# Up-projection pairs as blocks of seven half-size products in a two-layer encoder kernel

## The chip, the cores and the metric

The kernel runs on one core of one Trainium2 chip. The metric is the device time of one execution in microseconds (us). The core has a matrix engine (TensorE, PE in the profile, with its weight loads as PEld), three engines for elementwise work (VectorE is DVE, ScalarE is ACT, GpSimd is POOL), a queue that issues loads (SyncE, SP), on-chip memory (SBUF, 128 partitions), eight PSUM banks into which PE writes, and 16 DMA engines that move data between HBM and SBUF. The engines run side by side. Each works through its own instructions strictly in program order and waits on semaphores for the others.

## The reference, cut to what matters

Two post-norm layers over 512 tokens of width 1024. In each, a token part (attention, retention, gates, output projection, LN1) is followed by a channel part. The change lies in the channel part alone:

```python
def conv_glu_ffn(x, w_up, conv_w, conv_b, w_down):
    h = x @ w_up                       # (512, 1024) @ (1024, 5632)
    hp = jnp.pad(h, ((0, 0), (1, 1), (0, 0)))
    h = hp[:, :-2] * conv_w[0] + hp[:, 1:-1] * conv_w[1] + hp[:, 2:] * conv_w[2] + conv_b
    a, b = jnp.split(h, 2, axis=-1)
    return (jax.nn.gelu(a) * b) @ w_down
...
    ffn = conv_glu_ffn(x, ...)
    ple = jax.nn.sigmoid(x @ w_ple_gate[i]) * (p[i] @ w_ple_proj[i])
    x = layer_norm(ALPHA * x + ffn + ple, ln2_g[i], ln2_b[i])
```

`D_FF` is 2816, that is 22 tiles of 128 channels for the half `a` and 22 for the half `b`.

## The kernel before, in words

**Products in three parts.** Every f32 operand is kept as two rounded parts, `hi` and `lo` (`split`, L169: ScalarE copies the source into `hi`, VectorE subtracts to get `lo`). A product of two operands is three matmuls, hi·hi, hi·lo and lo·hi (`mm3`, L395).

**The weight stream.** All weights of a layer come as chunks of 128x1024 f32 (512 KB) in the order in which they are used (`Stream`, L275). A chunk is loaded by the SP queue (`fetch`), split by ScalarE and VectorE (`prep`), and used by PE (`get`). `get` splits ahead: up to `deep` (5) chunks beyond the one in use, of which at most three in all lie in the three rotating buffers of the pool `wsplit` (`N_W`), those marked as held lying in the large pool `unit` (30 buffers of 4 KB per partition). So the split of a chunk that lies three places later in those buffers has to wait until PE is done with the chunk in use. Loads are issued `LOOK` (3) chunks further ahead.

**Seven products for eight.** Some projections are computed by a Winograd form of Strassen's scheme: the weight is four blocks a, c, b, d, and seven products (kinds a, c, t1, t2, d, t3, t4) with sums of blocks replace eight. The sums of the weight are made by DMA: POOL issues a transfer that adds the next block onto a raw chunk in SBUF (`add`, L303). A raw chunk passes through a, t1, t2 and t4: each sum is added only after the chunk has been split for the kind before (`prep`, L362). Items marked `sent` (L352) make their `lo` in another way: ScalarE negates `hi`, and a POOL DMA adds the weight onto it. The sums of the activations are made by `vg_sums` (L673) on VectorE and ScalarE, eight `unit` buffers for four sums. In the token part `product_t` (L1078) does such a product in 24 matmuls of 128x256, for the gate blocks; in the channel part before the change, the gate of the per-layer input (`pg`, L1340) and the down projection (`products`, L1436) use the scheme with 128x512 matmuls, and the sums of x made for `pg` are dropped after it.

**The channel part.** The 22 pairs of up tiles come in three segments of 3, 4 and 4 pairs of tile numbers (`SEGS`), so 6, 8 and 8 tiles. For one tile, `up_tile` (L1266) runs two products `gemm_t` (one of half a, one of half b) with 24 matmuls of 128x512 each. After each comes a convolution: ScalarE scales the PSUM result into `ca`, VectorE adds the two neighbours with two instructions of 511 columns. Then ScalarE applies GELU and VectorE multiplies the halves. `up_step` (L1299) makes from two tiles the operands of the down projection: `a11` (128x256, from the even tile), `k2` (128x512, from the odd tile), and in `s_parts` (L1287) the two sums `sa` and `sb`, each split into hi and lo. For the last pair of a segment `s_parts` comes after the first down product (L1568).

After the up tiles of a segment come its seven down products in the order a, c, t1, t2, d, t3, t4, each of 24 matmuls (18 in the first segment), each of which reads one operand of every pair of the segment: a reads `a11` of pairs 0 to 3 in turn, c reads `k2`. Their results are added into the residual tiles `R` by VectorE (`into`).

**What sets the order.** In the channel part all five engines keep program order (`_Ordered.on = set(ORD)`, L1255). An instruction that waits holds up all that stand behind it on its engine. So the place at which the Python code emits an operation is the place at which its engine runs it:

```python
        half = []
        for ab in range(2):
            ps = gemm_t(xs)          # get(): splits of later chunks are emitted here
            ...                      # convolution of this half
```

Of the kernel before, what the change touches and what calls it, by code (L numbers as in the profile page):

```python
# [10 lines left out]
F32R = mybir.dt.float32r  # L11
AF = mybir.ActivationFunctionType
ALU = mybir.AluOpType
# [51 lines left out]
BOUND = ("p0", "t4a", "tr", "t4b", "p1")  # L65
VG_DEEP = 3
VG_EARLY = "d"
VG_HELD = (('0t1', '1t1', '0t2', '0c', '1t2', '1a', '1d', '1t3'), ('0a', '0c', '0t1', '1t1', '1t3', '1t2', '0t3', '0t2', '1d'))


# [46 lines left out]
def trunk(tc, wpack, x_nat, x_tr, head, p_tr, rpb, decay, ln_par, ln_col, conv, cos_t, sin_t, dist, xi_d, zd, mask, ident_d, out):  # L117
# [4 lines left out]
    with ExitStack() as es:  # L122
# [14 lines left out]
        def nm(s):  # L137
            cnt[0] += 1
            return f"{s}_{cnt[0]}"
# [7 lines left out]
        def tmp(s, n=512):  # L147
            return tp.tile([P, n], F32, tag="t", name=nm(s))
# [92 lines left out]
        def pg_items(l):  # L241
# [11 lines left out]
                    n += 1  # L253
            return out

        def plain_items(l, f):

            if f[0] in "qk":
                h = int(f[1])
                cs = [12 * (h // 2) + 8 + 2 * (h % 2) + "qk".index(f[0])]  # L260
            elif f[:2] == "ga":
                cs = [52 + int(f[2])]
            elif f[:2] == "bb":
                cs = [44 + int(f[2])]
            elif f == "vn":
                cs = range(32, 36)
            elif f == "xn":
                cs = []
            elif f[0] == "p":
                cs = [72 + int(f[1])]  # L270
            else:
                cs = [24 + 2 * int(f[2]) + "qk".index(f[1])]
            return [Item("w", (l, c, 0, 1024), 1024) for c in cs]

        class Stream:  # L275


            def __init__(self):
                self.seq = []
                for l in range(DEPTH):  # L280
                    tile = 0
                    plain = lambda c: self.seq.append(Item("w", (l, c, 0, 1024), 1024, pool=up if (l, c) in RESIDENT else None))
                    self.seq += vg_items(l)
                    self.seq += fill_items(l)
                    for c in range(60, 72):
                        plain(c)
                    self.seq += pg_items(l)
                    for s, n in enumerate(SEGS):
                        for c in range(UP0 + 2 * max(tile, PG.count("up")), UP0 + 2 * (tile + 2 * n)):
                            plain(c)  # L290
                        tile += 2 * n
# [362 lines left out]
        for l in range(DEPTH):  # L654
# [608 lines left out]
            for t in range(4):  # L1263
                nc.sync.dma_start(R[t], rscr[l][t * P:(t + 1) * P, :])

            def up_tile(i):  # L1266
                half = []
                for ab in range(2):
                    ps = gemm_t(xs)
                    ci = ab * NF + i  # L1270
                    a = tmp("ca")
                    nc.scalar.activation(a, ps, AF.Identity, bias=cw[:, ci, 3:4], scale=cw[:, ci, 1:2])
                    nc.vector.scalar_tensor_tensor(a[:, 1:], ps[:, :-1], cw[:, ci, 0:1], a[:, 1:], op0=ALU.mult, op1=ALU.add)
                    nc.vector.scalar_tensor_tensor(a[:, :-1], ps[:, 1:], cw[:, ci, 2:3], a[:, :-1], op0=ALU.mult, op1=ALU.add)
                    half.append(a)
                nc.scalar.activation(half[0], half[0], AF.Gelu_apprx_tanh)
                nc.vector.tensor_mul(half[0], half[0], half[1])
                return half[0]

            H1, H2 = slice(0, 256), slice(256, 512)  # L1280
            N1, N2 = slice(0, 512), slice(512, 1024)
            tile = 0
            a11, k2, sa, sb, sums = {}, {}, {}, {}, []
# [14 lines left out]

            def up_step(j, last_pair):  # L1299

                nonlocal tile
                p, g = j // 2, up_tile(tile)
                tile += 1
                if j % 2 == 0:
                    if p % 2 == 0:
                        a11p[0] = up.tile([P, 2, 2, 256], F32R, tag="u", name=nm("a11"))
                    a11[p] = a11p[0][:, p % 2]
                    split(a11[p][:, 0, :], a11[p][:, 1, :], g[:, H1])
                    sums.append([p, g])
# [3 lines left out]
                sums[-1].append(g)  # L1313
                if not last_pair:
                    s_parts(*sums.pop())

            a11p = [None]


            def ple_gate(t, c, src, scale):  # L1320
# [12 lines left out]
            def residual():  # L1333

                while late:
                    t = late.pop(0)
                    nc.scalar.activation(xn[t], xn[t], AF.Copy, scale=ALPHA)
                    nc.gpsimd.dma_start(R[t], xn[t], accum_op=ALU.add)

            def pg():  # L1340
# [6 lines left out]
                for key in PG:  # L1347
# [4 lines left out]
                    for k in S_AT:  # L1352
                        if k == name:
                            r = next(sg)
                            S = r if isinstance(r, dict) else S
                    if key == "up":
                        up_step(ups, False)
                        ups += 1
                        residual()
                        continue  # L1360
# [55 lines left out]
            pg()  # L1416
            st = [sp.tile([P, 2, 6], F32, tag="bn", name=nm("bn")) for _ in range(4)]
            for s, n in enumerate(SEGS):
                for j in range(tile - 2 * sum(SEGS[:s]), 2 * n):
                    up_step(j, j == 2 * n - 1)  # L1420
                    residual()
                fin = s == len(SEGS) - 1
                lhs = {
                    "a": lambda p, h, i: a11[p][:, h, i * P:(i + 1) * P],
# [140 lines left out]
                ws.deep = A_DEEP[s]  # L1565
                product("a", u, True)
                ws.deep = DEEP
                s_parts(*sums.pop())  # L1568
                if fin and not last:
                    ple_in(l + 1)  # L1570
                for i in range(2):
# [100 lines left out]
def _pack(w_in, w_ba, w_bb, w_out, w_up, w_down, w_pg, w_pp):  # L1672
    ch = []
    q_na, k_na, v_na, q_r, k_r, v_r, g_r, ga, gb = np.split(w_in, np.cumsum([512, 512, 512, 512, 512, 1024, 1024, 1024])[:], axis=1)
    vr, gr, qr, kr = _mov(v_r), _mov(g_r), _stat(q_r), _stat(k_r)
    for hp in range(2):
        ch += list(vr[hp]) + list(gr[hp])
        for h in (2 * hp, 2 * hp + 1):
            ch += [qr[h], kr[h]]
    qn, kn = _stat(q_na), _stat(k_na)  # L1680
    for m in range(4):
        ch += [qn[m], kn[m]]
    ch += list(_mov(v_na)[0])
# [10 lines left out]
    for i in range(NF):  # L1694
        ch += [su[i], su[NF + i]]
    ch += _blocks(w_down)
    assert len(ch) == NCH
    return np.stack(ch)
# [69 lines left out]
```

## Time and profile before

| | us |
|---|---|
| median of 3 runs (lowest, highest) | 1680.46 (1680.31, 1680.69) |
| span of the profiled execution (first to last instruction) | 1679.3 |
| PE busy | 1669.5 (99%) |
| VectorE busy | 1228.2 (73%) |
| ScalarE busy | 949.1 (57%) |
| POOL busy | 189.2 (11%) |
| all bytes moved by DMA | 289.68 MB, 172 GB/s on average |

The time of the profiled execution is not measured apart from its span; the span is 1.2 us under the median of the runs, which is what lies around it. The matmuls are pipelined: a record of a 128x512 matmul is 389 ns long, while the next one starts 227 ns after it. So durations of matmuls are not added up here, but starts are compared. On the other engines the records follow one another with little overlap, and a row's duration is close to its cost. "idle before <-" in a row names what ended the engine's wait.

In layer 0 the up tiles of the second segment run from 586 us to 673 us, its down products to 711 us, the up tiles of the third segment to 798 us.

### The profile page before, as it was taken

How to read it: one execution, taken by the hardware profiler on the slowest of the kernel's cores; microseconds unless marked ns; L12 is line 12 of the kernel's file. 1: busy time of each engine (PE TensorE's matmuls, PEld its weight loads, DVE VectorE, ACT ScalarE, POOL GpSimd, SP SyncE). 2: the span in 40 equal slices, each digit the busy share in tenths (PEclk: the TensorE clock that was granted, in tenths of full speed). 3: DMA queues.
4: the chain of work that ended last, by engine and by line, in shares of the span. 5: the costliest groups of instructions: out<-in, count | busy, mean ns of one | idle time of the engine just before them, and what ended most of it. 6: DMA issues, size and time to landing. Idle time of an engine off the chain costs nothing.

```text
span 1679.3 us, 22089 instructions
## 1 busy us (share of the span) xinstructions
PE 1669.5 (99%) x8325; PEld 1418.1 (84%) x8325; DVE 1228.2 (73%) x1857; ACT 949.1 (57%) x1418; POOL 189.2 (11%) x216
## 2 busy tenths in 40 slices
PE   9999999999999999999999999999999999999997
PEld 7889988888888888888888899888888888888886
DVE  6756676776787767757876566877688887676678
ACT  6765676853366535335476647668534574353354
POOL 1111111110200100100112011111002010000003
PEclk9999999999999999999999999999999999999999
DMA  8989666666655535535788795667667565265274
GB/s 303 249 234 233 171 149 139 165 173 223 207 135 161 121 112 163 135 111 172 193 231 219 184 245 163 138 144 170 160 241 225 130 171 126 88 181 132 89 212 101
DMA packets 87530, 289.68 MB, mean 172 GB/s; under 512 B 9984, under 2 KB 14592, under 8 KB 87424
## 3 DMA queue, kind: packets, MB, share of 16 engines
q1 hardware_dynamic: 62512, 199.66, 33.7%
q0 software_dynamic: 24912, 88.62, 30.2%
q8 instruction: 65, 1.06, 0.3%
q14 instruction: 41, 0.34, 0.1%
HBM read 269.36 MB, written 17.30 MB: 171 GB/s over the span
## 4 chain that ended last, share of the span: by engine, by line
PE 99%; DVE 1%; ACT 0%; POOL 0%; issue 0%; DVEq 0%; POOLq 0%; ACTq 0%
PE gt L90 31%; PE u L90 13%; PE v L90 7%; PE gt L397 6%; PE gt L398 6%; PE gt L399 6%; PE w L90 4%; PE gn L399 3%; PE gn L397 3%; PE gn L398 3%; PE x L90 1%; PE u L397 1%; PE u L399 1%; PE u L398 1%; PE gn L90 1%; PE na L1023 1%
## 5 line engine op out<-in xcount | busy, mean ns | idle before, releaser
L90 PE MATMUL gt<-x1t,hi 128*128 128x512 f32 x1408 | 433.5, 389 | 0.0
L90 PEld LDWEIGHTS gt<-x1t,hi 128*128 128x128 f32 x1408 | 264.3, 188 | 55.0
L90 PE MATMUL gt<-x1t,lo 128*128 128x512 f32 x704 | 274.1, 389 | 0.1
L90 DVE TENSOR_TENSOR lo<-raw,hi 128x1024 fp32r<-128x1024 f32 (+1 forms) x147 | 175.9, 1206 | 43.5 <-ACT hi L90 43.3
L90 DVE SCALAR_TENSOR_TENSOR ca<-gt,cw,ca 128x511 f32<-128x511 f32 x176 | 131.8, 749 | 78.5 <-ACT ca L90 75.4
L90 ACT CAST hi<-raw 128x1024 fp32r<-128x1024 f32 (+1 forms) x147 | 151.1, 1037 | 33.1 <-PE u L90 13.4
L90 PEld LDWEIGHTS gt<-x1t,lo 128*128 128x128 f32 x704 | 132.2, 188 | 28.1 <-DVE lo L90 1.0
L90 DVE TENSOR_TENSOR lo<-rawa,hi 128x1024 fp32r<-128x1024 f32 x94 | 109.8, 1176 | 49.3 <-ACT hi L90 48.9
L90 ACT ACTIVATE ca<-gt,cw 128x512 f32<-128x512 f32 x88 | 68.5, 779 | 131.7 <-PE gt L90 131.7
L90 ACT CAST hi<-rawa 128x1024 fp32r<-128x1024 f32 x94 | 94.3, 1014 | 39.0 <-DMA rawa<-in_wpack 16.5
L90 POOL DMA_DIRECT2D rawa<-in_wpack x72 | 65.0, 947 | 368.6 <-DVE lo L90 308.0
L397 PE MATMUL gt<-xt,hi 128*128 128x512 f32 x256 | 100.8, 394 | 0.0
L398 PE MATMUL gt<-xt,hi 128*128 128x512 f32 x256 | 99.8, 390 | 0.0
L399 PE MATMUL gt<-xt,lo 128*128 128x512 f32 x256 | 99.7, 389 | 0.0
L170 ACT CAST hi<-raw 128x1024 fp32r<-128x1024 f32 x44 | 45.8, 1050 | 76.2 <-PE gt L398 29.8
L355 ACT CAST hi<-raw 128x1024 fp32r<-128x1024 f32 x48 | 50.4, 1050 | 49.1 <-PE gt L398 41.2
L357 POOL DMA_DIRECT2D lo<-in_wpack x48 | 42.1, 876 | 294.7 <-ACT lo L356 215.4
L90 POOL DMA_DIRECT2D rawt<-in_wpack x20 | 18.8, 1004 | 381.0 <-DMA rawt<-in_wpack 364.8
L171 DVE TENSOR_TENSOR lo<-raw,hi 128x1024 fp32r<-128x1024 f32 x44 | 53.4, 1223 | 10.9 <-ACT hi L170 10.7
L399 PEld LDWEIGHTS gt<-xt,lo 128*128 128x128 f32 x256 | 48.1, 188 | 10.3
L90 PE MATMUL v<-hi,sa 128*128 128x512 f32 x176 | 56.1, 389 | 0.0
L397 PEld LDWEIGHTS gt<-xt,hi 128*128 128x128 f32 x256 | 48.2, 188 | 9.1
(348 smaller groups left out, 4216.9 us busy)
## 6 DMA issues: line engine op xcount, KB each, us to landing
raw<-in_wpack SPq DMA_DIRECT2D x235, 512.0 KB, 3.7
rawa<-in_wpack POOLq DMA_DIRECT2D x84, 512.0 KB, 6.6
lo<-in_wpack POOLq DMA_DIRECT2D x48, 512.0 KB, 5.5
rawa<-in_wpack SPq DMA_DIRECT2D x28, 512.0 KB, 6.8
rawt<-in_wpack SPq DMA_DIRECT2D x28, 512.0 KB, 6.5
rawt<-in_wpack POOLq DMA_DIRECT2D x28, 512.0 KB, 7.2
r_scr<-pp SPq DMA_DIRECT2D x8, 512.0 KB, 10.1
gb<-gb_scr SPq DMA_DIRECT2D x8, 512.0 KB, 5.0
```

The lines of the kernel that those rows point to most:

```text
L90: r = f(*a, **k)
L170: nc.scalar.copy(hi, src)
L171: nc.vector.tensor_sub(lo, src, _f(hi))
L355: nc.scalar.copy(hi[:, cs], it.raw[:, cs])
L357: nc.gpsimd.dma_start(lo[:, cs], wpack[l, c][:, o:o + w], accum_op=ALU.add)
L397: nc.tensor.matmul(ps, lh, rh, start=start, stop=False, skip_group_check=more)
L398: nc.tensor.matmul(ps, lh, rl, start=False, stop=False, skip_group_check=more)
L399: nc.tensor.matmul(ps, ll, rh, start=False, stop=stop, skip_group_check=more)
L1023: nc.tensor.matmul(ov[kt], lv, pt[kt // 2][:, sp_, c], start=i == 0 and sp_ == 0, stop=i == 3 and sp_ == 1)
```

## The change

In the second and third segment of each layer, three of the four pairs of up tiles become blocks (`_up_blocks`): both tiles of a pair and both halves, that is a 1024 x 512 weight, are multiplied by the seven products of `product_t` with 24 matmuls of 128x256 each, instead of by four `gemm_t` of 24 matmuls of 128x512. The fourth pair stays as it was. The seven products of the three blocks interleave: a block starts seven places after the one before, its kinds two places apart (`_up_order`):

```
0a 0c 0t1 0t2 1a 0d 1c 0t3 1t1 0t4 1t2 2a 1d 2c 1t3 2t1 1t4 2t2 p 2d 2t3 2t4 p
```

where p is a plain tile. The weights are repacked to match. Kinds c, t2 and t3 are held in the pool `unit`, kind d is `sent`. The results are put together in two `unit` buffers `uh` per block by ScalarE copies (a, t1, t2, t4) and VectorE sums (c, d, t3). The convolution then reads SBUF, not PSUM. It is a generator (`up_conv`) of which one step is emitted after each block product that is not a t4; what is left of it by the last plain tile is emitted between that tile's two products and its own convolution (`drain(between)`). The sums of x from `pg` stay in SBUF to the end of the up tiles (`Sx`), eight of the 30 `unit` buffers.

```diff
+KINDS = ("a", "c", "t1", "t2", "d", "t3", "t4")
+UP_SENT = ("d",)
+UP_HELD = ("c", "t2", "t3")
+def _up_order(s):
+    if s == 0:
+        return ["p"] * (2 * SEGS[0] - PG.count("up"))
+    n = SEGS[s] - 1
+    at = [(2 * j + len(KINDS) * b, f"{b}{k}") for b in range(n) for j, k in enumerate(KINDS)]
+    end = 2 * (len(KINDS) - 1) + len(KINDS) * (n - 1)
+    return [k for _, k in sorted(at + [(end - 5, "p"), (end + 1, "p")])]
...
+        def up_items(l, s):
+            t0, by = 2 * sum(SEGS[:s]), {}
+            for b, t in enumerate(_up_blocks(s)):
+                pos = {(q, 0): (l, UP0 + 2 * t + i, 0, 1024) for i, q in enumerate("acbd")}
+                for it in block_items(pos, {k: up for k in UP_HELD}, VG_EARLY, 1):
+                    it.sent = it.kind in UP_SENT
+                    by[f"{b}{it.kind}"] = [it]
...
+            def conv3(ci, h):
+                a = tmp("ca")
+                nc.scalar.activation(a, h, AF.Identity, bias=cw[:, ci, 3:4], scale=cw[:, ci, 1:2])
+                nc.vector.scalar_tensor_tensor(a[:, 1:], h[:, :-1], cw[:, ci, 0:1], a[:, 1:], op0=ALU.mult, op1=ALU.add)
+                nc.vector.scalar_tensor_tensor(a[:, :-1], h[:, 1:], cw[:, ci, 2:3], a[:, :-1], op0=ALU.mult, op1=ALU.add)
+                return a
-            def up_tile(i):
-                half = []
+            def up_tile(i, between=None):
+                half, ps = [], []
                 for ab in range(2):
-                    ps = gemm_t(xs)
...
+                    ps.append(gemm_t(xs))
+                    if between is None:
+                        half.append(conv3(ab * NF + i, ps[ab]))
+                if between is not None:
+                    drain(between)
+                    half = [conv3(ab * NF + i, ps[ab]) for ab in range(2)]
...
+            def up_conv(i, j, h):
+                for f in range(2):
+                    a = conv3(i + f, h[0][:, f])
+                    yield
+                    b = conv3(NF + i + f, h[1][:, f])
+                    nc.scalar.activation(a, a, AF.Gelu_apprx_tanh)
+                    yield
+                    nc.vector.tensor_mul(a, a, b)
+                    yield from placed(j + f, a, False)
...
+            def up_block(b, kind):
+                if kind == "a":
+                    bh[b] = [unit_f("uh", (P, 2, 512)) for _ in range(2)]
+                    bu[b] = bank("u")
+                    product_t(kind, bu[b], True)
+                    nc.scalar.copy(bh[b][0][:, :, H1], v3(bu[b]))
+                elif kind == "c":
+                    w = bank("w")
+                    product_t(kind, w, True)
+                    nc.vector.tensor_add(bh[b][0][:, :, H1], bh[b][0][:, :, H1], v3(w))
...
+                elif kind == "t2":
+                    product_t(kind, bu[b], False)
+                    nc.scalar.activation(bh[b][1][:, :, H1], v3(bu[b]), AF.Copy, scale=-1.0)
...
-                for j in range(tile - 2 * sum(SEGS[:s]), 2 * n):
-                    up_step(j, j == 2 * n - 1)
-                    residual()
+                for k in _up_order(s):
+                    if k == "p":
+                        end = t + 1 == t0 + 2 * n
+                        up_step(t, t - t0, end, (x for g in late_conv for x in g) if end else None)
+                        t += 1
+                        residual()
+                        continue
+                    up_block(int(k[0]), k[1:])
+                    if k[1:] == "t4":
+                        b = int(k[0])
+                        late_conv.append(up_conv(_up_blocks(s)[b], 2 * b, bh.pop(b)))
+                    elif late_conv and next(late_conv[0], 0) == 0:
+                        late_conv.pop(0)
```

More of the change, by code (lines that the diff above doesn't have):

```diff
@@ L67, with _up_blocks @@
 VG_EARLY = "d"
+KINDS = ("a", "c", "t1", "t2", "d", "t3", "t4")
[8 more added lines that the diff above has]
+    return [k for _, k in sorted(at + [(end - 5, "p"), (end + 1, "p")])]
+def _up_blocks(s):
+    t0 = 2 * sum(SEGS[:s])
+    return [t0 + 2 * b for b in range(SEGS[s] - 1)] if s else []
 VG_HELD = (('0t1', '1t1', '0t2', '0c', '1t2', '1a', '1d', '1t3'), ('0a', '0c', '0t1', '1t1', '1t3', '1t2', '0t3', '0t2', '1d'))
@@ L288, in __init__ @@
                     for s, n in enumerate(SEGS):
-                        for c in range(UP0 + 2 * max(tile, PG.count("up")), UP0 + 2 * (tile + 2 * n)):
-                            plain(c)
-                        tile += 2 * n
+                        self.seq += up_items(l, s)
                         items = down_items(l, s)
@@ L1312, in up_step @@
                 split(k2[p][:, 0, :], k2[p][:, 1, :], g)
[L1313 to L1317, printed above, removed]
+                if last_pair:
+                    sums["last"] = p, sums.pop(p), g
+                    yield
+                    return
+                yield
+                s_parts(p, sums.pop(p), g)
+                yield
+            def up_step(t, j, last_pair, between=None):
+                drain(placed(j, up_tile(t, between), last_pair))
+            a11p = {}
             def ple_gate(t, c, src, scale):
@@ L1567, in trunk @@
                 ws.deep = DEEP
-                s_parts(*sums.pop())
+                s_parts(*sums.pop("last"))
                 if fin and not last:
@@ L1693, in _pack @@
     su = _stat(w_up)
-    for i in range(NF):
-        ch += [su[i], su[NF + i]]
+    blocks = [t for s in range(len(SEGS)) for t in _up_blocks(s)]
+    for i in range(0, NF, 2):
+        if i in blocks:
+            w = w_up.reshape(2, 4, P, 2, NF // 2, 256)
+            ch += [w[int(k in "cd"), :, :, int(k in "bd"), i // 2].transpose(1, 0, 2).reshape(P, 1024) for k in "acbd"]
+        else:
+            ch += [su[i], su[NF + i], su[i + 1], su[NF + i + 1]]
     ch += _blocks(w_down)
```

56 lines of the change are left out of this document (37 added, 19 removed).

## The prediction

> **What bounds the kernel now.** I read the page's busy times and chain first, then the sums over stretches of time.
>
> ```profile
> span 1679.3 us, 22089 instructions
> PE 1669.5 (99%) x8325; PEld 1418.1 (84%) x8325; DVE 1228.2 (73%) x1857; ACT 949.1 (57%) x1418; POOL 189.2 (11%) x216
> PE 99%; DVE 1%; ACT 0%; POOL 0%; issue 0%; DVEq 0%; POOLq 0%; ACTq 0%
> ```
>
> ```profile
> core 0: us, PE busy (x) PEld busy (x) DVE busy (x) ACT busy (x) POOL busy (x), PEclk, DMA share, GB/s
> 586.00:673.00 87.00, 87.00 (x385) 72.03 (x385) 60.22 (x81) 39.79 (x54) 3.45 (x4) 1.00 0.45 138
> 673.00:711.00 38.00, 38.00 (x170) 31.45 (x169) 26.81 (x34) 15.23 (x17) 3.48 (x4) 1.00 0.57 132
> ```
>
> PE is the bound throughout: the chain is 99% PE. In the up stage (first row) VectorE is idle for 27 of 87 us. Nothing makes PE wait, so fewer matmul microseconds are a gain only while the others keep up.
>
> **What PE gains.** The chain in order of time gives the pace of 128x512, and the records of one gate block's product that of 128x256:
>
> ```profile
> 659.87 13.60 PE gt L90 x60
> 673.47 5.44 PE u L90 x24
> 678.91 5.44 PE w L90 x24
> ...
> 689.79 5.44 PE u L90 x24
> ...
> 711.55 3.63 PE gt L90 x16
> ```
>
> ```profile
> L397 PE MATMUL w<-xt,hi x16: 283/283/283, 120.4 to 125.8; 128*128 128x256 f32 x16
> ```
>
> 5.44/24 is 0.227 us. Of the second, the first and last start lie 45 matmuls apart (every third is of this line): 5.4/45 = 0.120. A pair is now 96 x 0.227 = 21.8 us, a block 168 x 0.120 = 20.2. That is 1.6 us for each of 12 blocks: **-19 us**. The Trainium skill (TensorE: Matmul & The Clock Gate, Part 1, the section on the fixed cost per matmul) gives N/2.4 GHz plus about 2.5 ns between starts; by that a block would save 96 x 215.8 - 168 x 109.2 ns = 2.4 us, 28 in all. The rows here are slower for both sizes, and they decide.
>
> **The work that has to keep up.** A pair splits 4 chunks, a block 7, of which six cost VectorE 1.2 us each and the sent one only ScalarE; three sums of 0.69 come on top, the convolution stays: about +4.5 us of VectorE per block. Spread evenly it fits (the 27 us idle, three blocks). It is not spread evenly.
>
> **The tail of convolutions.** These rows are VectorE's end of the second segment's up tiles; the second fence is ScalarE:
>
> ```profile
> 663.61 1.53 DVE L90 SCALAR_TENSOR_TENSOR ca<-gt,cw,ca 128x511 f32<-128x511 f32 x2
> 665.25 0.69 DVE L90 TENSOR_TENSOR ca<-ca,ca 128x512 f32<-128x512 f32 x1
> 666.41 0.42 DVE L90 TENSOR_TENSOR a<-ca,a 128x256 fp32r<-128x256 f32 x1 [0.47 <-ACT a L90]
> ...
> 668.88 1.54 DVE L90 SCALAR_TENSOR_TENSOR ca<-gt,cw,ca 128x511 f32<-128x511 f32 x2 [0.29 <-ACT ca L90]
> ...
> 671.46 2.35 DVE L90 TENSOR_TENSOR lo<-raw,hi 128x1024 fp32r<-128x1024 f32 x2
> 674.32 1.54 DVE L90 SCALAR_TENSOR_TENSOR ca<-gt,cw,ca 128x511 f32<-128x511 f32 x2 [0.50 <-ACT ca L90]
> 675.96 0.69 DVE L90 TENSOR_TENSOR ca<-ca,ca 128x512 f32<-128x512 f32 x1
> 677.34 0.69 DVE L90 TENSOR_TENSOR k<-ca,k 128x512 fp32r<-128x512 f32 x1 [0.69 <-ACT k L90]
> 678.29 2.36 DVE L90 TENSOR_TENSOR lo<-rawa,hi 128x1024 fp32r<-128x1024 f32 x2 [0.26 <-ACT hi L90]
> 680.57 0.42 DVE L90 TENSOR_TENSOR ta<-ca,ca 128x256 f32<-128x256 f32 x1
> ...
> 683.42 0.68 DVE L90 TENSOR_TENSOR sb<-tb,sb 128x512 fp32r<-128x512 f32 x1
> ...
> 686.52 1.23 DVE L90 TENSOR_TENSOR lo<-rawa,hi 128x1024 fp32r<-128x1024 f32 x1 [1.22 <-ACT hi L90]
> ```
>
> ```profile
> 668.07 0.78 ACT L90 ACTIVATE ca<-gt,cw 128x512 f32<-128x512 f32 x1 [0.73 <-PE gt L90]
> ...
> 685.43 1.05 ACT L90 CAST hi<-rawa 128x1024 fp32r<-128x1024 f32 x1 [2.13 <-DMA rawa<-in_wpack]
> ```
>
> Today the last product's weights start to be split when PE ends the product before (668.07); three splits end at 673.8, the last convolution runs from 674.3, and `k2` of the last pair is complete at 678.03. Product c needs it with its 16th matmul, at 678.91 + 15 x 0.227 = 682.3. PE has 4.3 us in hand.
>
> In the changed kernel's program order, a block's convolution has seven steps and an eighth call that only finds it finished. Block 0 uses all eight from 1t2 to 2d, so block 1 gets one step (at 2t3), and the rest of block 1 and all of block 2 are drained after the last plain tile's products, behind the three splits that wait, as now, for PE to end the product before. Their price, from the rows: a pair of neighbour sums 1.5; from the second half's sums to the end of `a11` 663.6 to 666.8, 3.2; from there to the end of `k2` 674.3 to 678.0, 3.7; `s_parts` 680.57 to 684.10, 3.5. A whole block is 1.5 + 3.2 + 1.5 + 3.7 + 3.5 = 13.4, the rest of block 1 is 11.9. The last tile's first half (1.5) moves behind them, so the splits end earlier, at 672.6. Reading SBUF instead of PSUM may save a few hundredths per row; I take none.
>
> On the clock of the rows: `k2` of the last pair comes at 672.6 + 11.9 + 13.4 + 5.2 = 703.1, 25.1 us later than now. `a11` of block 2 comes at 672.6 + 11.9 + 4.7 = 689.2; product a wants it at 673.47 + 12 x 0.227 = 676.2. PE thus waits 13 us in a, and 20.8 in all until c has `k2`. After that the chain is as now but 25.1 - 20.8 = 4.3 us later: t2's weight, ready at 687.75 and wanted at 690.0, has 2.3 in hand, so 2.0 more are lost. That is 22.8 us in each of four segments: **+91 us**. Lower bound: without any wait between ScalarE and VectorE (3.7 us in the two blocks), 25.1 becomes 21.4 and the loss is 17 per segment, 68. Upper bound 25.1 per segment, 100, if no slack is in hand.
>
> **The head of each block stage.** Block 0's chunk passes a, t1, t2 with no other block between, and each step waits for a DMA sum.
>
> ```profile
> 706.14 1.06 ACT L90 CAST hi<-raw 128x1024 fp32r<-128x1024 f32 x1 [1.67 <-PE u L90]
> ```
>
> ```profile
> 708.04 1.22 DVE L90 TENSOR_TENSOR lo<-raw,hi 128x1024 fp32r<-128x1024 f32 x1
> ```
>
> ```profile
> 679.82 0.86 POOL L90 DMA_DIRECT2D rawa<-in_wpack  x1 [7.11 <-DVE lo L90]
> ```
>
> The first up chunk's split is tied to PE's start of the last down product, since its buffer comes free there, and its `lo` ends at 709.3 (second row). From a POOL issue to the next split is 679.82 to 685.43, 5.6 us; from there to the end of `lo` (687.75) 2.3; to the next issue 0.3. So t1 is split by 717.5 and t2's `hi` starts at 723.4. ScalarE stands there, and behind it in its queue are 1a's split and the copy of 0a out of PSUM, which t2 overwrites: 723.4 + 1.05 + 1.05 + 0.7 = 726.2. PE starts the stage at 711.55 and wants 0t2 three products (8.6 us) later, at 720.2: 6.0 us lost. In the second segment the last down product has 18 matmuls, not 24, so it is 1.4 more. **+27 us** for four.
>
> Then 0d. Behind 0t2's split, POOL issues four sums in a burst (0t4, 0t3, 1t1, d's `lo`).
>
> ```profile
> q1 hardware_dynamic: 62512, 199.66, 33.7%
> q0 software_dynamic: 24912, 88.62, 30.2%
> ```
>
> ```profile
> rawt<-in_wpack POOLq DMA_DIRECT2D x28, 512.0 KB, 7.2
> lo<-in_wpack POOLq DMA_DIRECT2D x48, 512.0 KB, 5.5
> ```
>
> 0t3's sum is issued at about 727 and lands 7.2 later; ScalarE waits for it and, behind that, copies out 0t1, which 0d overwrites: 735.9, against 0d's turn at 732.0. At least 3.9 us. By the second row a summing chunk takes 0.302 x 1679/88.62 MB x 0.524 MB = 3.0 us of all DMA engines (a plain load 1.5), so four end no earlier than 738: up to 7. I take 5: **+20 us**. Both ends: 0 if the slack of PE's earlier wait hides it, 28.
>
> **Nothing for the rest.** The bytes: per block 4 loads and 5 sums, 6 + 15 = 21 us of DMA against 20.2 of PE, hidden once PE waits anyway; without those waits it costs 12 x 0.8 = 10. The eight buffers kept cost loads a wait on PE, hidden by three chunks of lead; if not, it is in the upper end. ScalarE's extra work per block (three casts and a negation of 1.05, four copies of up to 0.78: 7 us) fits in its idle half.
>
> **Sum.** 1679.3 - 19 + 91 + 27 + 20 = 1798 for the span; the runs' median is 1.2 above the span, so about **1800 us**.
>
> **Rivals.**
> *Faster.* The matmuls are all that counts: 1680 - 19 = 1661. This is so if VectorE's added work between the last split and `k2` stays under the 4.3 us in hand; the order of the instructions puts 25 there. A leftover of under half a block's convolution would decide for it.
> *The tail alone.* The head is hidden, as the chunks of block 0 are split earlier than I read: 1680 - 19 + 91 = 1752. For it: the chain of sums never held PE in the gate blocks. Against: there other products lie between.
> *The clock falls.* PE's last record ends at 1670.9 (the row of `u<-xw`), and the granted clock stands third from the right in the sums over the last stretches:
>
> ```profile
> 1669.00:1674.00 5.00, 1.86 (x9) 1.20 (x7) 4.75 (x9) 1.74 (x4) 4.76 (x5) 1.00 0.80 214
> 1674.00:1679.30 5.30, 0.00 (x0) 0.00 (x0) 1.78 (x3) 0.00 (x0) 0.59 (x2) 0.67 0.48 181
> ```
>
> ```profile
> 1665.71 5.15 PE L90 MATMUL u<-xw,k 128*128 128x512 f32 x22
> ```
>
> ```profile
> 1.20 4.02 PE L504 MATMUL warm<-warm 128*128 128x512 bf16 x9 [1.20 <-DVE warm L501]
> 4.82 3.02 PE L90 MATMUL gn<-hi,ptr 128*128 128x512 f32 x8
> ```
>
> 0.67 in the mean: a fall to half 4.9 us after the last matmul. At the start nine matmuls of 512 columns took 4.02 us and the next eight 3.02, so coming back costs about 5 us at half pace, 2.5 lost. Three waits per segment are of that size: 12 x 2.5 = 30, to 1830. I take none, since most of it is inside the next wait. The Trainium skill states this rule (same page, Part 1): an idle window of about 3.4 us halves the clock, a busy one restores it.
> *Buffers and bursts.* Sums at 10 us instead of 5.6 (two in the head's chain) and loads waiting for buffers: about 40 more, 1840.
> *No change* would need losses to equal 19 us by chance.
>
> **Chances.** The forecast 0.55, the tail alone 0.2, the clock 0.1, buffers 0.1, faster 0.04, same 0.01. The range 1725 to 1850 takes in the lower bound of the tail with the head hidden (1680 - 19 + 68 = 1729) and both upper rivals. Slower by over 0.2% (about what a measurement of this kernel can tell from no change) is 0.95.
>
> **What would show it.** PE's waits go from 1 us to over 100: about 13 us on `a11` (pair 2) in product a, 8 on `k2` in c, in the up stage on 0t2 and 0d. A block's product takes 2.9 us. VectorE runs without a pause for about 30 us around the end of the up tiles. The prediction is wrong if the leftover convolutions run before the last splits, or if PE's waits lie elsewhere.

## The result, and the profile after

The changed kernel takes 1904.3 us (median of 4 runs, 1900.4 to 1906.5), the kernel before 1680.4: a ratio of 1.133 (95% interval 1.131 to 1.135). Slower was forecast, but at 1800 us with an upper end of 1850; 104 us are missing in the forecast.

The page's span and busy times of the changed kernel:

```profile
span 1904.8 us, 24180 instructions
PE 1716.1 (90%) x9189; PEld 1486.7 (78%) x9189; DVE 1278.4 (67%) x1917; ACT 1021.8 (54%) x1514; POOL 242.1 (13%) x276
PEclk9999999999998897898999999999999998988988
```

PE is idle for 189 us of the span where it was idle for 10. VectorE, with 50 us more to do, has a lower share than before (67% for 73%): no engine is full. The last row, the granted clock in 40 slices, falls in the channel parts of both layers.

The sums over stretches show where. In order: the first segment's down products, the second segment's block stage, the end of its last tile with its down products (the third segment looks like the second). Columns as in the prediction's rows.

```profile
560.00:592.00 32.00, 24.16 (x98) 19.14 (x98) 25.10 (x37) 17.03 (x22) 3.48 (x4) 0.89 0.62 157
592.00:705.00 113.00, 91.26 (x595) 85.80 (x594) 51.89 (x63) 44.16 (x56) 15.70 (x18) 0.89 0.67 159
705.00:776.00 71.00, 50.10 (x194) 39.13 (x193) 52.51 (x73) 30.51 (x40) 5.21 (x6) 0.86 0.43 104
```

PE had no pause in these stages before; the first stretch, in the kernel before:

```profile
560.00:592.00 32.00, 32.00 (x143) 26.50 (x142) 22.95 (x33) 12.68 (x17) 2.59 (x3) 1.00 0.50 126
```

Now it pauses in every one of them, also in the first segment, whose up tiles the edit leaves plain. In the block stage VectorE is busy for less than half of the time.

PE's waits, summed by what released them (total, times, longest):

```profile
PE u L111 <- ACT a L111: 49.0, 8, 11.2
PE w L111 <- ACT k L111: 36.8, 6, 7.3
PE u L111 <- ACT uh L111: 22.2, 4, 6.5
PE v L111 <- DMA lo<-in_wpack: 21.3, 9, 3.7
PE v L111 <- ACT uh L111: 18.5, 4, 5.9
PE u L111 <- DVE uh L111: 9.7, 4, 2.6
PE u L111 <- DVE lo L111: 5.8, 8, 0.8
PE u L111 <- ACT ca L111: 5.0, 3, 2.9
PE v L111 <- ACT hi L111: 3.8, 2, 2.7
PE u L111 <- ACT hi L111: 2.7, 2, 1.4
PE v L111 <- DVE lo L111: 2.2, 4, 0.8
```

The first two rows are `a11` and `k2` in the down products a and c; six waits on `k2` in two layers mean that the first segment has one too. The rows with `uh`, `lo<-in_wpack` and `ca`, and `ACT hi` and `DVE lo` on `v`, are the block stages: 82.7 us. `DVE lo` and `ACT hi` on `u` are the weight of down product t2.

A first account of the 225 us between the two spans: 19 less for the products by the forecast, 179 more in which PE is idle (177 in the eleven rows above). What remains, about 65 us, is not a wait in this view; it goes with the lower clock (0.950 granted in the mean, 0.999 before). That is a remainder, not a measurement. Whether it is a cause is tested below.

### The profile page after: what moved, and what is told of

Its sections match the earlier page's. It is cut to its first block, busy times and chain, and to the rows that moved or that the text cites. A ratio compares the mean times of both kernels' runs of the same rounds, so it can differ in the third digit from the quotient of the medians.

```text
span 1904.8 us, 24180 instructions
## 1 busy us (share of the span) xinstructions
PE 1716.1 (90%) x9189; PEld 1486.7 (78%) x9189; DVE 1278.4 (67%) x1917; ACT 1021.8 (54%) x1514; POOL 242.1 (13%) x276
## 5 line engine op out<-in xcount | busy, mean ns | idle before, releaser
L111 DVE TENSOR_TENSOR lo<-rawa,hi 128x1024 fp32r<-128x1024 f32 (+1 forms) x142 | 168.0, 1192 | 191.3 <-ACT hi L111 191.1
L111 ACT CAST hi<-rawa 128x1024 fp32r<-128x1024 f32 (+1 forms) x142 | 143.6, 1025 | 172.2 <-DMA rawa<-in_wpack 121.6
L111 PE MATMUL gt<-x1t,hi 128*128 128x512 f32 x640 | 197.2, 389 | 0.0
L111 PEld LDWEIGHTS gt<-x1t,hi 128*128 128x128 f32 x640 | 119.6, 188 | 24.4
L111 PE MATMUL gt<-x1t,lo 128*128 128x512 f32 x320 | 124.7, 390 | 0.1
L111 PE MATMUL u<-x1t,hi 128*128 128x256 f32 x384 | 77.8, 303 | 14.7 <-DVE uh L111 9.7
L111 PE MATMUL v<-sh,lo 128*128 128x256 f32 x192 | 61.8, 322 | 23.6 <-DMA lo<-in_wpack 21.3
L111 PE MATMUL v<-sh,hi 128*128 128x256 f32 x192 | 60.9, 317 | 22.3 <-ACT uh L111 18.5
L111 PEld LDWEIGHTS u<-x1t,hi 128*128 128x128 f32 x384 | 66.4, 211 | 16.2 <-issue 12.3
L111 PE MATMUL u<-sh,hi 128*128 128x256 f32 x192 | 58.7, 306 | 22.2 <-ACT uh L111 22.2
L111 DVE SCALAR_TENSOR_TENSOR ca<-gt,cw,ca 128x511 f32<-128x511 f32 x80 | 59.3, 748 | 23.5 <-ACT ca L111 22.1
```

The lines of the kernel that those rows point to most:

```text
L111: r = f(*a, **k)
```

## The experiments

Each run is compared with the kernel before on the same chip (1680.4 to 1680.8 us in the four groups). "The changed kernel" stands at 1.133.

### The first segment: its last tile as before

The changed kernel also emits the first segment's last tile in the new order (both products, then both convolutions). This run takes that away.

```diff
-up_step(t, t - t0, end, (x for g in late_conv for x in g) if end else None)
+up_step(t, t - t0, end, (x for g in late_conv for x in g) if end and late_conv else None)
```

> The changed kernel (1904 us), but the last up tile of the first segment, which has no blocks, runs its convolutions as in the kernel before: the first half's right after its product, ahead of the next chunk's split. Theory of the order of instructions: PE's two waits of about 8 us on `k2` in product c of the first segments (at 565 and 1513 us in the changed kernel's trace) come from that move alone, so they go, with some 2 us of matmuls at half clock behind each: 2 x 10 = 20 us, about 1884. Rival, the eight sum buffers kept in SBUF cause the waits by keeping loads back: nothing changes, 1904.

1901.2 us, ratio 1.131 (1.129 to 1.133). The wait on `k2` in the first segment stayed, 6.8 us at the longest in place of 7.3. The new order of that tile is not what makes `k2` late; this theory fell, and the kept buffers came next.

### The kept buffers alone

The kernel before, with the eight buffers of the sums of x held until the last segment's down products by reads of one column each, and nothing else changed.

```diff
+fin = s == len(SEGS) - 1
+if fin:
+    for k in ("t1", "t2", "t3", "d"):
+        for x in kept_S[k]:
+            nc.vector.tensor_copy(small("hold", 1), _f(x[:, 0, :1]))
```

> The kernel before (1680 us), with one part of the change alone: the eight buffers with the sums of x are kept to the end of the up tiles, by eight one-column copies per layer that read them there (some 16 x 0.07 = 1 us of VectorE). Theory of the order of instructions: no more than 0.2%, 1680 to 1683. Rival, the missing buffers hold back loads: PE waits appear in the second and third up stage, 10 us or more, 1690 and over.

1718.4 us, ratio 1.022 (1.021 to 1.024): 38 us with no block in the kernel. The reads themselves are not it: 16 at 0.15 us each, 2.3 us of VectorE in all. The three largest of PE's waits in this run:

```profile
PE w L90 <- ACT k L90: 13.5, 2, 6.7
PE u L90 <- ACT hi L90: 6.9, 2, 3.9
PE u L90 <- DVE lo L90: 2.8, 5, 0.8
```

The first row is the first segment's `k2` in both layers, as in the changed kernel. ScalarE ahead of it, first in the kernel before, then in this run:

```profile
557.90 0.78 ACT L90 ACTIVATE ca<-gt,cw 128x512 f32<-128x512 f32 x1 [3.44 <-PE gt L90]
...
561.39 0.62 ACT L90 CAST k<-ca 128x512 fp32r<-128x512 f32 x1 [0.76 <-DVE ca L90]
```

```profile
560.27 1.05 ACT L90 CAST hi<-raw 128x1024 fp32r<-128x1024 f32 x1 [11.29 <-PE u L90]
...
564.12 0.80 ACT L90 ACTIVATE ca<-gt,cw 128x512 f32<-128x512 f32 x1
...
571.52 0.62 ACT L90 CAST k<-ca 128x512 fp32r<-128x512 f32 x1 [1.46 <-DVE ca L90]
```

ScalarE stands for 11.3 us at the split of a weight chunk until PE lets go of something, and the convolution of the last tile is behind it in the queue. `k2` is 10.1 us later. In the changed kernel the same split stands for as long:

```profile
560.02 1.05 ACT L111 CAST hi<-raw 128x1024 fp32r<-128x1024 f32 x1 [11.30 <-PE u L111]
```

The split needs a place for its result; that this is a buffer of the `unit` pool is what the next two runs test.

### Four buffers instead of eight

```diff
-    for k in ("t1", "t2", "t3", "d"):
+    for k in ("t1", "t2"):
```

> The kernel before with four of the eight sum buffers kept (those of t1 and t2) instead of eight, which cost 38 us (1718). Theory: what the kept buffers cost is a shortage with a threshold, the first segment's held chunks wait for a buffer only when fewer than some number is left; four buffers are then nearly free: 1680 to 1690 us and no 7-us wait on k2 in the first segment. Rival: each buffer taken costs its share of the loads' lead, half of the loss remains: about 1699 us.

1680.9 us, ratio 1.0003 (0.9993 to 1.0012). In the whole kernel PE waits only at its start, for the warm-up operand. Four buffers cost nothing, eight cost 38 us: a threshold somewhere between them, not a share per buffer.

### Eight buffers, and fewer held chunks

The kernel before with eight buffers kept; in the first segment product a's split chunks go to the three rotating buffers, which leaves four more in the pool.

```diff
-HELD = {3: ("a", "c"), 4: ("c",)}
+HELD = {3: ("c",), 4: ("c",)}
```

> The kernel before with all eight sum buffers kept (1718 with the held chunks as they are), but in the first segment only product c's split chunks are held in the same pool, not a's, which leaves four buffers more there. Theory: it is the held chunks of the down products that find no buffer, ScalarE stands at their split and all behind it is late; 1680 to 1695 us, no 7-us wait on k2. Rival: a's chunks in the three rotating buffers make PE wait as long in another place, or the shortage lies in the later segments too; 1710 us or more.

1702.0 us, ratio 1.013 (1.011 to 1.014). The `k2` row is gone, and 16 of the 38 us with it. So in the first segment it was the split of a held chunk that found no buffer. The waits for t2's weight stay, 8.8 us on its `hi` and 3.9 on its `lo`, 12.7 of the remaining 22 us. Which buffer is short there was not tried; both theory and rival were half right.

### The waits of the tails filled

In each tail PE gets products with a zero weight that add nothing, in front of the matmuls that wait: 48 in product a, 34 in c.

```diff
+for _ in range({("a", 1, 0, 0): 48, ("c", 1, 1, 0): 34}.get((kind, j, kk, i), 0) if s else 0):
+    nc.tensor.matmul(ps[i], zero, _ap(zero, 0, [[0, 4], [1, P]]), start=False, stop=False, skip_group_check=True)
```

> The changed kernel, with matmuls of zero weights added into product a (48, before its second chunk) and product c (34, before the last pair) of the second and third segments. They add zero to what is there, so nothing of the computation is left out; at about 0.22 us each they fill 10.5 and 7.5 us in which PE waits in the changed kernel. Theory of the clock: PE's granted clock stays at 1.00 through the tails, and what the half clock costs there, by the trace 4.2 to 5.2 us of slow matmuls per segment, is saved: up to 18 us, 1886. Rival: the slow matmuls between the waits are hidden by the next wait, so the clock is full but the time stays within 8 us of 1904. If the waits are not of VectorE's making but PE's own, the time grows by 4 x 18 = 72.

1903.3 us, ratio 1.132 (1.130 to 1.134), the changed kernel's time within the intervals. The granted clock in the first tail rose from 0.86 to 0.95 (third number from the right):

```profile
705.00:776.00 71.00, 65.19 (x273) 44.75 (x273) 52.48 (x73) 30.63 (x40) 5.21 (x6) 0.95 0.42 103
```

PE's waits on `a11` fell from 49.0 to 7.5 us and those on `k2` in the tails went, as their place is filled; the wait on t2's weight (`PE u <- ACT hi`) rose from 2.7 to 9.3. Faster matmuls only bring PE earlier to an operand that is no earlier.

### The waits of the block stages filled

The same in front of 0t1, 0t2, 0d, 1d and 2t4, into a PSUM bank that nothing reads.

```diff
+fill({"0t1": 12 if s == 1 else 0, "0t2": 20, "0d": 36, "1d": 5, "2t4": 10}.get(f"{b}{kind}", 0))
```

> The changed kernel with products of a zero weight (bf16, 128x512, into a PSUM bank of their own, read by nothing) in front of 0t1, 0t2, 0d, 1d and 2t4 of each stage, somewhat fewer than PE waits there now, so that PE does not stand idle. Theory: the granted clock of the block stages goes from 0.87 to about 1.0, and the 30 us by which their matmuls run slow come off: 1875 to 1885 us. Rival: as in the tails, PE only comes earlier to its next wait, which grows; the time stays within 5 us of 1904.

1898.5 us, ratio 1.130 (1.128 to 1.132): 6 us less. The clock of the first block stage is nearly full now (0.89 in the changed kernel):

```profile
592.00:705.00 113.00, 103.65 (x686) 88.62 (x685) 52.47 (x63) 45.37 (x58) 15.73 (x18) 0.98 0.68 160
```

In both places the rival was right in the main: of the 20 to 30 us that the theory expected here 6 came, where the rival allowed 5. The slow matmuls are real, but most of the time is set by operands that come late on other engines.

### Two convolution steps for each block product

```diff
-elif late_conv and next(late_conv[0], 0) == 0:
-    late_conv.pop(0)
+else:
+    for _ in range(2):
+        if late_conv and next(late_conv[0], 0) == 0:
+            late_conv.pop(0)
```

> The changed kernel, but two steps of the convolution are emitted after each block product that is not a t4, not one. By the order, block 1 then has all but its `s_parts` (3.5 of the 11.9 us) behind it before the last plain tile, so VectorE's tail before the last `k2` is 8.4 us shorter. Theory of the tail: PE's waits in products a and c fall from about 19 to about 11 us in each of four segments, 4 x 8.4 = 34 us less, about 1870, a little more if less of the time is at half clock. Rival, the tail's wait is for DMA sums or buffers and not for VectorE's queue: it stays near 19 us per segment, 1904. Second rival: the denser convolutions delay the block stage by as much as the tail gains, 1904 with the waits moved.

1908.4 us, ratio 1.135 (1.134 to 1.137). The leftover of the tail did move, and two of PE's waits grew:

```profile
PE u L111 <- ACT hi L111: 25.9, 6, 6.3
PE u L111 <- DVE uh L111: 23.5, 4, 5.9
```

The wait on `a11` falls from 49.0 to 15.6 us, but those on a split and on the sum of 2t3, mostly in the stage itself, rise from 2.7 and 9.7 to 25.9 and 23.5. The first block stage is 9.5 us longer (from its first matmul to the first of down product a: 124.2 for 114.7) and the down products behind it 8.6 shorter (56.9 for 65.5): the steps delay what stands behind them on ScalarE and VectorE there by as much as they help later.

### VectorE's part of the drained convolutions taken out

The neighbour sums of the convolutions that are drained after the last plain tile's products (seven pairs per segment) are left out; the rest stays.

```diff
+light.append(1)
 drain(between)
+light.clear()
...
+if not light:
     nc.vector.scalar_tensor_tensor(a[:, 1:], ...)
     nc.vector.scalar_tensor_tensor(a[:, :-1], ...)
```

> The changed kernel without the neighbour sums of the convolution in the part that is drained after the last plain tile's products (seven of them per segment; this part of the computation is left out), the scaling, GELU, multiplication, splits and sums there as they were. Theory: the wait of the down products is VectorE's work, each pair of neighbour sums 1.5 us, so 10.6 us go per segment: 1862 us, PE's wait in a falls from 13 to about 5 us and that in c from 6 to about 3. Rival: the handing over between ScalarE and VectorE sets the pace; less than half of it goes, 1885 us or more.

1872.7 us, ratio 1.115 (1.113 to 1.116).

```profile
PE u L111 <- ACT a L111: 28.6, 4, 7.2
PE w L111 <- ACT k L111: 26.0, 6, 7.2
```

The time falls by 31.6 us for 42 us of VectorE's work taken out, three quarters. In the tail VectorE's work is the main cause, as forecast. That the last quarter is the handing over to ScalarE and back is argued, not shown.

### Kind d split like the others

```diff
-UP_SENT = ("d",)
+UP_SENT = ()
```

> The changed kernel with kind d split like every other chunk (its lo by VectorE, not by a POOL transfer that adds the weight onto a negated hi). Theory: PE's waits on that lo (21.3 us in 9 times in the changed kernel) are the landing time of the POOL transfer behind the sums issued before it, so they go, and 1885 to 1890 us remain. Rival: the chunk is only one of several things that are late there; VectorE has 1.2 us more per block, the waits move to the copies of 0d and the sums of 2t3, and the time stays within 4 us of 1904.

1902.9 us, ratio 1.133 (1.131 to 1.134): no change. The row `DMA lo<-in_wpack` (21.3) is gone, and in its place stand:

```profile
PE u L111 <- ACT ca L111: 13.7, 4, 6.6
PE u L111 <- DVE uh L111: 13.3, 5, 2.9
PE v L111 <- DVE uh L111: 13.1, 6, 3.4
```

The POOL transfer for d was the last to arrive, but the next things were as late.

### A plain tile between 0c and 0t1

```diff
-return [k for _, k in sorted(at + [(end - 5, "p"), (end + 1, "p")])]
+return [k for _, k in sorted(at + [(3, "p"), (end + 1, "p")])]
```

> The changed kernel with the first plain tile of each block stage moved from between 2t2 and 2d to between 0c and 0t1. Theory: the waits of 0t2 (4.7 to 6.8 us in each of four stages, 22 in all) come from the chain of sums on block 0's chunk with too little other work between; 5.4 us of plain tile cover it and they go, the waits of 0d shrink by up to the same clock time: 1880 to 1885 us. Rival: the waits move to the end of the stage, where 2d, 2t3 and 2t4 now follow one another without the tile between, and the convolution steps are not the less: 1900 to 1910 us.

1859.2 us, ratio 1.106 (1.105 to 1.108), 45 us less, twice what was expected. The expectation counted 5.4 us for the tile, which is one of its two products; PE has 10.9 us of work in it. The row of 0t2 (`PE u <- ACT uh`, 22.2) is gone; that of 0d fell from 18.5 to 4.4, while d's `lo` rose from 21.3 to 26.5 and the two rows of `DVE uh` are 12 higher together. So other work between the steps of block 0's chunk takes away PE's wait in both places; that it is the sums that have to be covered, the next run shows.

### The sums of the weight taken out

The block weights t1, t2, t3 and t4 are used as loaded; the POOL transfers that make the sums are left out. Loads, splits, products, copies and the sent `lo` of d stay.

```diff
 it.sent = it.kind in UP_SENT
+it.plus = None
...
 def add(self, it):
+    if it.plus is None:
+        return
```

> The changed kernel without the DMA sums of the block weights: t1, t2, t3 and t4 of each block are multiplied with the chunk as it was loaded, so this part of the computation is left out; the loads, splits, products, copies and the sent lo of d stay. Theory: ScalarE stands at the splits of chunks whose sum has not landed (28 us on the first chunk of a block and 9 on t3's in the second segment's stage) and the copies that PE waits for are behind them; without the sums PE's waits in the block stages fall from 22 us each to under 10, and 1830 to 1855 us remain. Rival: the splits, copies and rotating buffers set the pace and the waits only change their names; 1885 us or more.

1803.4 us, ratio 1.073 (1.072 to 1.075): 101 us less, more than the 50 to 75 expected and the largest step of all runs with three blocks. All of PE's waits of this run over 3 us in total:

```profile
PE u L111 <- ACT a L111: 49.0, 8, 11.2
PE w L111 <- ACT k L111: 36.0, 6, 7.3
PE u L111 <- DVE uh L111: 9.4, 4, 2.6
PE u L111 <- DVE lo L111: 4.7, 8, 0.8
```

The tails and the first segment are as they were; of the 82.7 us of the block stages the row of 2t3's sum is left (9.4) and 0.7 on d's `lo`. The four block stages take 347 us in place of 449 and 348 in the kernel before. What holds them is in the main the sums. The run takes out the wait for each sum and its load on the DMA engines together (the plain loads of the first block stage land after 3.6 us in the median, 5.8 with the sums), and the two are not separated. ScalarE's queue in the changed kernel, with POOL's issues behind it, shows how:

```profile
612.00 1.99 ACT L111 CAST hi<-rawa 128x1024 fp32r<-128x1024 f32 x2 [7.48 <-DMA rawa<-in_wpack]
613.89 0.58 ACT L111 COPY uh<-u 128x512 f32<-128x512 f32 x1
...
626.02 1.04 ACT L111 CAST hi<-rawt 128x1024 fp32r<-128x1024 f32 x1 [8.58 <-DMA rawt<-in_wpack]
626.97 0.59 ACT L111 ACTIVATE uh<-v 128x512 f32<-128x512 f32 x1
```

```profile
606.22 0.86 POOL L111 DMA_DIRECT2D rawa<-in_wpack  x1 [9.16 <-DVE lo L111]
614.60 0.86 POOL L111 DMA_DIRECT2D rawa<-in_wpack  x1 [7.52 <-DVE lo L111]
615.14 1.22 POOL L111 DMA_DIRECT2D rawt<-in_wpack  x1
...
616.80 1.36 POOL L111 DMA_DIRECT2D lo<-in_wpack  x1
```

ScalarE stands 7.5 us at t2's split until the sum has landed, and the copy of 0a that 0t2 waits for comes behind it; then 8.6 us at t3's, and behind that the copy of 0t1 that 0d waits for.

### One block per segment

One block instead of three, its products among the plain tiles, its convolution finished two tiles before the end, four steps after each plain tile, and the last tile as in the kernel before.

```diff
+return ["0a", "0c", "p", "0t1", "p", "0t2", "0d", "p", "0t3", "0t4", "p", "p", "p"]
...
-return [t0 + 2 * b for b in range(SEGS[s] - 1)] if s else []
+return [t0] if s else []
```

> The changed kernel with one block per segment instead of three, its products among the plain tiles (0a 0c p 0t1 p 0t2 0d p 0t3 0t4 p p p), its convolution finished two tiles before the end, and the last tile as in the kernel before. Theory: the tail and the head go with the order, what is left is the price of the eight buffers (38 us alone) less four blocks of 1.6 us: 1710 to 1715 us. Rival: a block's seven chunks and five sums cost waits wherever it stands; 1740 us or more.

1781.2 us, ratio 1.059 (1.058 to 1.061): the rival was right. The `a11` wait of the tails is gone, but 0t4 now waits for the sum of 0t3 right before it (`PE u <- DVE uh`, 15.4 us in four times), and the last plain tile of the stage for its split (`PE gt <- ACT hi`, 12.0 in four). With product a's chunks no longer held in the first segment as well:

> The kernel with one block per segment, and in the first segment only product c's split chunks held, not a's. Theory: the buffers' price goes too, as far as it goes in the kernel before with eight buffers kept and the same edit; 1674 to 1690 us, at best 6 us under the kernel before. Rival: the waits stay, and the time is that of the one-block kernel without the edit, within 5 us.

1764.8 us, ratio 1.051 (1.049 to 1.052). The edit is worth 16 us here as in the kernel without blocks. Four blocks would save PE 6 us by the forecast's price, and with the kept buffers the kernel is still 84 us slower in this order; 22 of these the kernel without blocks pays too (1702.0). Where the rest arises was not tested. No version here beats the kernel before.

## Why the prediction was right in direction and wrong in size

The length of each stage, from the start of its first matmul to that of the next stage's, shows where the miss lies (us, both layers; the last stage of all runs to the end of the span):

| stage | before | after | more | forecast |
|---|---|---|---|---|
| down products of the first segments (2) | 57.1 | 77.7 | 20.6 | 0 |
| block stages (4) | 348.2 | 449.2 | 101.0 | 28 (27 + 20 - 19) |
| down products of the other segments, the "tails" (4) | 155.5 | 259.8 | 104.3 | 91 |
| sum | | | 226 | 119 |

The spans differ by 225.5, and the forecast for the span was 119 more. So 73 us of the miss of 107 lie in the block stages, 21 in the first segments and 13 in the tails.

**What PE gains: as forecast.** The two rows are the first matmuls of two successive block products: 24 matmuls of 128x256 in 2.87 us, 0.120 each.

```profile
595.97 0.40 PE L111 MATMUL u<-x1t,hi 128*128 128x256 f32 x2
...
598.84 0.40 PE L111 MATMUL w<-x1t,hi 128*128 128x256 f32 x2
```

The 19 us that follow from it are in no run by themselves: even without the sums the block stages take 347 us, 1 less than before.

**The tail: right up to c, t2's weight mis-sized.** Forecast were 13 us in a, 20.8 until c has `k2`, 2.0 for t2's weight. The rows of the second segment:

```profile
712.55 0.50 PE L111 MATMUL u<-hi,a 128*128 128x512 f32 x1 [1.05 <-ACT a L111]
...
726.12 0.79 PE L111 MATMUL u<-hi,a 128*128 128x512 f32 x1 [11.21 <-ACT a L111]
726.72 0.63 PE L111 MATMUL u<-lo,a 128*128 128x512 f32 x1
727.14 1.05 PE L111 MATMUL u<-hi,a 128*128 128x512 f32 x2
...
730.32 0.39 PE L111 MATMUL u<-hi,a 128*128 128x512 f32 x1
730.55 0.39 PE L111 MATMUL w<-hi,k 128*128 128x512 f32 x1
...
739.88 0.79 PE L111 MATMUL w<-hi,k 128*128 128x512 f32 x1 [5.77 <-ACT k L111]
```

12.3 in a, 5.8 in c, 18.0 together. Over all four tails the `a11` row and the `k2` row without the first segments' two (36.8 less 2 x 7.3) give 71.2, 17.8 each; t2's two rows (8.5) give 2.1 each. The waits leave out what the slow matmuls between them take. By the starts, c's 16th matmul comes 29.2 us after the stage's start (710.66 to 739.88), where the prediction's 673.47 and 682.3 are 8.8 apart: 20.4 later, for 20.8 forecast. Taking VectorE's work out (31.6 of 42 us) confirms that cause. Behind that matmul each tail loses 4 to 7 us more, where the forecast had 2.0 for t2's weight. The kernel before with eight buffers kept loses 17 us in these same stages without any block, so the buffers may be the reason; that was not separated.

**The head: right in kind, mis-sized at 0d, and it ended too early.** By the starts of the products, against 2.87 us for each product before them, 0t2 comes 32 us late in the four stages (forecast 27) and 0d another 28 (forecast 20). The first link of the chain took 7.3 us from issue to split (596.20 to 603.47) and the second 5.8 (606.22 to 612.00), for 5.6 priced. For 0d the step that failed is "0t3's sum is issued at about 727 and lands 7.2 later": of the burst of four, t3's sum took 10.9 us to the split (615.14 to 626.02). The larger failure is that nothing behind 0d's start has a term, and half of the loss is there: 60 of the 120 us that the four stages lose against the bare products. There PE waits for d's `lo` (21.3 us in all; in block 0 a transfer of the same burst, which landed later still), at 1t4 (5.0) and at 2t4 for 2t3's result (9.7), and its matmuls are slow behind the waits. Taking the sums out shortens the four stages by 102, where the head's term was 47. The rival "buffers and bursts" had the mechanism (10 us for 5.6), but only in the head's chain, and was given 0.1.

**"Nothing for the rest": wrong.** This is the other step that failed: "the eight buffers kept cost loads a wait on PE, hidden by three chunks of lead". They cost 38 us alone, 21 of them in the first segments, where the changed kernel loses the same 21. It was no load that waited: a held chunk's split found no free buffer and stopped ScalarE's queue with a convolution in it. "If not, it is in the upper end" put at most 40 us for buffers and bursts together.

**The clock: taken at nothing, and nearly so.** The rows above show it: after the wait of 11.2 us matmuls start 0.42 us apart (726.72 to 727.14), and 4.2 us after the wait's end 0.23 apart again (730.32 to 730.55). The Trainium skill (TensorE: Matmul & The Clock Gate, Part 1) says that an idle window of about 3.4 us halves the clock and a busy one of that length restores it; the trace agrees, with half the pace after 11.2 us of idle time and full pace within 4.2 us. But filling the waits brought the clock back and not the time, in the tails (1.132 for 1.133) and hardly in the block stages (1.130). "Most of it is inside the next wait" was right; the rival of 1830 was not.

**VectorE's capacity: right, and beside the point.** VectorE was to fit if its work were spread, and it is busy for 51.9 of 113 us in the block stage. It waits for as long:

```profile
DVE lo L111 <- ACT hi L111: 51.9, 16, 7.8
```

Added up, the sums make 55 of the block stages' 73 us (102 less the 47 that were priced); the other 18 are lost without them too. The first segments' 21 are the kept buffers' price, with about the same wait on `k2` and the same length (77.7 us for 77.6) as in the old kernel with eight buffers kept. The tails' 13 are not assigned.

## What to carry to other kernels

Where engines keep program order, ask of each added instruction what it may have to wait for and which copies, splits or convolutions stand behind it; busy shares say nothing of that, and here VectorE and ScalarE were busy for 67% and 54% while the kernel lost 13%. A chain of transfers that each wait for the step before needs other work between its links for the whole of its time (here 10.0 and 8.4 us from one issue to the next), and that work has to lie on the engine that would otherwise wait. Buffers kept longer can be free up to a threshold and then stop a queue (here four cost nothing and eight 38 us); hold them in the old kernel, alone, before building on them.

## What the runs showed of the hardware that was not expected

Accumulating POOL transfers of 512 KB that are issued in a burst land one after the other. In the first block stage the two issued alone at 596.20 and 606.22 landed after 7.2 and 5.8 us; the four issued between 614.60 and 616.80, in this order t4's, t3's, the next block's t1 and d's `lo`, after 6.0, 10.9, 13.1 and 14.5 us. In the third segment's stage the last three of the same burst took 11.0, 13.2 and 14.8. The median of the three `lo` in the first block stage is

```profile
lo<-in_wpack POOLq DMA_DIRECT2D x3, 512.0 KB, 9.8
```

where over the whole kernel before it is 5.5. The other two, issued at 648.50 and 677.39, took 6.9 and 9.8, so being issued alone does not always make one fast. The DMA engines' mean share in that stage was 0.67.

The clock's fall to half (matmuls 0.42 us apart for 0.23) costs little time by itself where the next operand is late anyway: two kernels with PE kept running through its waits took 1903.3 and 1898.5 us, the one without 1904.3.
